# Scan of a hybrid Mamba/Hyena block: two products per group made by four scaled ACT copies instead of one POOL multiply

## The chip, the cores and the metric

One core of a Trainium2 chip runs the whole kernel as one program. Its engines work side by side, each through its own queue in order: PE (TensorE, matmuls), DVE (VectorE), ACT (ScalarE), POOL (GpSimd) and SP, which issues most transfers. The metric is the device time of one execution in microseconds (us), as the median of several runs; less is better.

## The reference

The reference is one layer on 1024 latent tokens of width 1024, with 256 context tokens: an input projection, a bidirectional chunked state-space scan (SSD) and a gated long convolution (Hyena) side by side, an output projection, and a retrieval over 16384 single-neuron experts. The change lies in the scan, which is, per direction and cut to what matters:

```python
xdt = (x * dt[..., None]).reshape(bsz, nc, q, g, r, p)
a_cum = jnp.cumsum(a, axis=-1)
l_intra = jnp.exp(segsum(a))
y_diag = jnp.einsum('bclgn,bcsgn,bgrcls,bcsgrp->bclgrp', cc, bc, l_intra, xdt)
...
y_off = jnp.einsum('bclgn,bcgrpn,bgrcl->bclgrp', cc, prev_states, jnp.exp(a_cum))
...
y = y + xs * d_skip
return group_rmsnorm(y * jax.nn.silu(z), norm_g, SSD_GROUPS)
```

There are 16 heads of 64 columns in 4 groups, and the latent tokens make 8 chunks of 128.

## The kernel before

Class `Ssd` does the scan. `run` goes through 32 steps, one for each of 4 groups in each of 8 chunks, and in each step runs `first` of the new group beside `second` of the group before.

`first` makes what `second` needs. A matmul gives the 128x128 product of the group's B and C (`cb`, in the PSUM tile `pe`). The tile `s_e`, which SP loads in `load_cum` (L559, three buffers), holds the cumulated decays of four heads in two directions, spread over all partitions; ACT subtracts and takes the magnitude head by head (L610, eight instructions a group) and then the exponential of all of it (L616). POOL makes `s_xd`, the inputs times their steps `dt`, for four heads at once, one instruction for each direction (L611, two buffers), and the skip term `s_y`, the inputs times `dskip` (L619, one buffer for a chunk). DVE masks `cb` (L617).

`second` multiplies `s_e` by the masked product on DVE (L632 and L634), has PE multiply it with `s_xd` (L639, into the PSUM tile `py`, one buffer), scales the part from the earlier states (L644, L647), adds everything into `s_y` (L648, L649) and multiplies it by the gate `s_z` on POOL (L650). After the fourth group of a chunk `done` advances the state (POOL's L503 among it), takes squares on ACT (L664), the root (L58), scales the rows (L668, a copy on ACT with a scale from a tile) and stores `s_y` (L669, to `d_ossd`). The next chunk's skip term can be written only when that store has landed.

The scan doesn't run alone. In `front` it is drawn along step by step beside the last slabs of the input projection (matmuls L199, weight split L50 and POOL's L51, convolution L229 and L235, transposes L245 with their copies L246 into `stage`), and in `mix` beside the long convolutions (matmuls L850 into the PSUM tiles `hx` and `hy`, DVE lines 766 to 845 and 993, ACT copies L777 to L823) and the key products (L1076, copied out by ACT in L1078). The order of the instructions on every engine is made by a scheduler that takes the work by priorities and simulates it; it isn't written in the code. `MB = 2` gives the projection two PSUM buffers.

Of the kernel before, what the change touches and what calls it, by code (L numbers as in the profile page):

```python
# [15 lines left out]
AF = mybir.ActivationFunctionType  # L16
# [413 lines left out]
class Ssd:  # L430
# [159 lines left out]
    def first(self, c, g, loaded):  # L590

        K, nc, wk, ps = self.K, self.K.nc, self.wk, self.ps
        x, b, bt, ct, z, prev, y = loaded
        gs = slice(g * 256, (g + 1) * 256)
        cb = ps.tile([128, 4, 128], F32, name="pe", bufs=PB)[:, 0]
        nc.tensor.matmul(cb, bt[:, g, :], ct[:, g, :], start=True, stop=True)
        e = self.e.pop(0)
        if 4 * c + g + 1 < 4 * NB:
            self.e.append(self.load_cum(4 * c + g + 1))
        xd = wk.tile([128, 2, 256], F32, name="s_xd", bufs=2)  # L600
        cbm = wk.tile([128, 2, 128], F32, name="s_cb", bufs=2)
        self.out = e, xd, cbm
        for d in range(2):
            h0 = d * 16 + g * 4
            if AD:
                (nc.vector if AD == 1 else nc.gpsimd).tensor_add(
                    e[:, d], e[:, d], self.ncum[:, c, h0:h0 + 4, None].to_broadcast([128, 4, 128]))
            else:
                for h in range(4):
                    nc.scalar.activation(e[:, d, h], e[:, d, h], AF.Abs, bias=self.ncum[:, c, h0 + h:h0 + h + 1])  # L610
            nc.gpsimd.tensor_mul(self.heads(xd[:, d]), self.heads(x[:, gs]),  # L611
                                 K.dt[:, c, h0:h0 + 4, None].to_broadcast([128, 4, 64]))
            yield
        if AD:
            nc.scalar.activation(e, e, AF.Abs)
        nc.scalar.activation(e, e, AF.Exp, scale=-1.0)  # L616
        nc.vector.tensor_mul(cbm, cb[:, None, :].to_broadcast([128, 2, 128]), self.tri)  # L617
        yield
        nc.gpsimd.tensor_mul(self.heads(y[:, gs]), self.heads(x[:, gs]),  # L619
                             self.dskip[:, g * 4:g * 4 + 4, None].to_broadcast([128, 4, 64]))  # L620
        yield

    def second(self, c, g, loaded, made):
# [1316 lines left out]
```

## Time and profile before

| what | value |
| --- | --- |
| median of 3 runs | 4127.27 us (4127.11 to 4129.32) |
| profiled execution, its own time | 4128.36 us |
| span of the profiled execution | 4126.3 us |
| mean granted TensorE clock | 0.964 |
| busy over the span: PE, DVE, ACT, POOL | 92%, 82%, 34%, 49% |

The span is the profiled execution from its first to its last instruction; a share is busy time over the span, over all stages together. The scan's groups take about a twelfth of the span, and the shares there are others than these.

### The profile page before, as it was taken

What the parts mean: (1) busy time and instruction counts of PE and PEld (TensorE: products, weight loads), DVE (VectorE), ACT (ScalarE), POOL (GpSimd) and SP (SyncE); (2) the same over time, 40 slices, a digit from 0 to 9 for tenths busy, and PEclk for the clock granted to TensorE, in tenths of its full rate; (3) what the DMA queues carried; (4) which work ended last, traced back from release to release, by engine and by line L of the source; (5) the groups of instructions that cost most, each with busy time, mean ns of one, the idle gap of its engine ahead of it and who ended that gap; (6) DMA issues with size and microseconds to landing.
All of it is one profiled execution on the core that took longest, in us unless ns stands there. A gap on an engine that the chain in (4) does not pass through costs nothing.

```text
span 4126.3 us, 60371 instructions
## 1 busy us (share of the span) xinstructions
PE 3781.7 (92%) x21993; PEld 3322.5 (81%) x21993; DVE 3394.6 (82%) x5997; ACT 1391.5 (34%) x2674; POOL 2038.8 (49%) x1643
## 2 busy tenths in 40 slices
PE   5999999999889999689999985999999999999996
PEld 3787887777788898479999985888888888788885
DVE  5666787555899787479999997799888889899897
ACT  3233333325554121232325676222322222222221
POOL 2232233244443221137524444677777777677776
PEclk9999999999799999789999998999999999999998
DMA  6333333366776445747727756799999899999997
GB/s 207 109 126 105 117 128 129 111 198 182 244 230 222 149 133 146 228 169 286 257 99 235 226 165 200 283 356 340 366 341 349 324 336 349 343 351 361 340 335 260
DMA packets 510921, 973.07 MB, mean 236 GB/s; under 512 B 33739, under 2 KB 291199, under 8 KB 506144
## 3 DMA queue, kind: packets, MB, share of 16 engines
q1 hardware_dynamic: 396864, 556.21, 40.6%
q0 software_dynamic: 110880, 405.98, 26.6%
q10 hardware_dynamic: 2880, 7.03, 0.5%
q8 instruction: 173, 2.83, 0.3%
q14 instruction: 124, 1.02, 0.1%
HBM read 822.15 MB, written 146.95 MB: 235 GB/s over the span
## 4 chain that ended last, share of the span: by engine, by line
PE 44%; DVE 22%; DMA 9%; issue 7%; POOL 5%; ACT 3%; SPq 0%; POOLq 0%; DVEq 0%; ACTq 0%
PE x_acc L1682 12%; PE x_s L1636 10%; PE mm L199 7%; DVE rows L1536 3%; PE pe L1134 2%; PE hy L850 2%; POOL rows L1512 2%; DMA s_e<-d_cum 2%; DMA x_vr<-in_peer_v_dram 2%; DVE r_e L1459 2%; PE tp L850 2%; DVE r_e L1457 2%; DMA rows<-in_peer_v_dram,ids 1%; PE hx L850 1%; DVE e_p L1549 1%
## 5 line engine op out<-in xcount | busy, mean ns | idle before, releaser
L1636 PE MATMUL x_s<-fTh,x_uh 128*128 128x320 f32 x2048 | 639.2, 312 | 14.3 <-ACT x_a L1637 14.1
L1636 PE MATMUL x_s<-fTh,x_ul 128*128 128x320 f32 x2048 | 637.1, 311 | 5.5 <-DVE x_ul L1597 5.5
L1636 PE MATMUL x_s<-fTl,x_uh 128*128 128x320 f32 x2048 | 636.9, 311 | 0.0
L1682 PE MATMUL x_acc<-x_vl,x_ah 128*128 128x512 f32 x1280 | 509.2, 399 | 28.0 <-POOL x_vl L1608 27.9
L1549 DVE SCALAR_TENSOR_TENSOR e_p<-rows,e_a,e_p 128x1024 f32<-128x1024 f32 x381 | 489.8, 1286 | 39.2 <-DMA rows<-in_peer_v_dram,ids 32.4
L1682 PE MATMUL x_acc<-x_vh,x_al 128*128 128x512 f32 x1280 | 506.5, 397 | 0.0
L1512 POOL DMA_INDIRECT rows<-in_peer_u_dram,ids x384 | 417.4, 1087 | 177.7 <-DVE rows L1536 48.3
L1536 DVE SCALAR_TENSOR_TENSOR rows<-rows,e_p 128x1024 f32<-128x1024 f32 x384 | 456.1, 1210 | 34.1 <-DMA rows<-in_peer_u_dram,ids 32.9
L1682 PE MATMUL x_acc<-x_vh,x_ah 128*128 128x512 f32 x1280 | 442.4, 397 | 38.3 <-DVE x_o L1688 16.8
L1512 POOL DMA_INDIRECT rows<-in_peer_v_dram,ids x384 | 402.4, 1048 | 140.4 <-DVE e_p L1549 62.5
L1636 PEld LDWEIGHTS x_s<-fTh,x_uh 128*128 128x128 f32 x2048 | 387.1, 189 | 30.2 <-ACT x_a L1637 19.9
L1636 PEld LDWEIGHTS x_s<-fTh,x_ul 128*128 128x128 f32 x2048 | 386.8, 189 | 15.5 <-DVE x_ul L1597 6.9
L1608 POOL TENSOR_TENSOR x_vl<-x_vr,x_vh 128x512 fp32r<-128x512 f32 x256 | 342.9, 1342 | 107.2 <-ACT x_vh L1607 103.8
L1636 PEld LDWEIGHTS x_s<-fTl,x_uh 128*128 128x128 f32 x2048 | 386.9, 189 | 9.1
L1682 PEld LDWEIGHTS x_acc<-x_vh,x_ah 128*128 128x128 f32 x1280 | 238.8, 190 | 90.5 <-DVE x_o L1688 23.1
L1682 PEld LDWEIGHTS x_acc<-x_vl,x_ah 128*128 128x128 f32 x1280 | 244.5, 191 | 81.0 <-POOL x_vl L1608 37.0
L1682 PEld LDWEIGHTS x_acc<-x_vh,x_al 128*128 128x128 f32 x1280 | 243.8, 190 | 47.9
L1597 POOL TENSOR_TENSOR x_ul<-x_raw,x_uh 128x1024 fp32r<-128x1024 f32 x57 | 140.1, 2457 | 281.5 <-ACT x_uh L1596 281.2
L1607 ACT ACTIVATE x_vh<-x_vr 128x512 fp32r<-128x512 f32 x256 | 159.9, 628 | 338.5 <-DMA x_vr<-in_peer_v_dram 265.7
L1596 ACT ACTIVATE x_uh<-x_raw 128x1024 fp32r<-128x1024 f32 x128 | 135.4, 1057 | 409.1 <-PE x_s L1636 362.3
L199 PE MATMUL mm<-xh,whi 128*128 128x512 f32 (+1 forms) x784 | 265.0, 413 | 7.4 <-DVE acc L235 3.6
L199 PE MATMUL mm<-xl,whi 128*128 128x512 f32 (+1 forms) x784 | 263.9, 411 | 7.6 <-DVE xl L51 7.6
(386 smaller groups left out, 8710.9 us busy)
## 6 DMA issues: line engine op xcount, KB each, us to landing
x_raw<-in_peer_uT_dram SPq DMA_DIRECT2D x128, 512.0 KB
x_vr<-in_peer_v_dram SPq DMA_DIRECT2D x256, 256.0 KB
d_G<-r_st SPq DMA_DIRECT2D x20, 2048.0 KB
x_g<-d_G SPq DMA_DIRECT2D x32, 1280.0 KB
wraw<-in_w_mod_dram SPq DMA_DIRECT2D x32, 1024.0 KB
wraw<-in_w_in_dram SPq DMA_DIRECT2D x24, 1024.0 KB
wk_w<-d_WK SPq DMA_DIRECT2D x24, 1024.0 KB
d_kr<-h_k SPq DMA_DIRECT2D x32, 512.0 KB
```

The costliest lines, as they stand in the source:

```text
L199: nc.tensor.matmul(p, w[:, k], x[j][:, k, t0:t0 + n], start=(k == 0 and q == 0), stop=(k == 7 and q == 2))
L850: nc.tensor.matmul(out, self.m[mats][:, tl, :], x, start=(n == 0), stop=(n == len(terms) - 1))
L1134: nc.tensor.matmul(p, a[:, k], w[:, ss], start=(k == 0 and q == 0), stop=(k == n - 1 and q == 2))
L1512: nc.gpsimd.indirect_dma_start(out=r, out_offset=None, in_=table, in_offset=bass.IndirectOffsetOnAxis(ap=ids[:, j:j + 1], axis=0))
L1536: nc.vector.scalar_tensor_tensor(r, r, 1.0, f, op0=ALU.mult, op1=ALU.mult, accum_out=d[:, j:j + 1])
L1549: nc.vector.scalar_tensor_tensor(acc, r, a[:, j:j + 1], acc, op0=ALU.mult, op1=ALU.add)
L1596: nc.scalar.activation(hi, raw, AF.Copy)
L1597: self.pace = (nc.vector if self.turn('u', UR if self.n < NE else UP) else nc.gpsimd).tensor_sub(lo, raw, hi.bitcast(F32)).ins
L1607: nc.scalar.activation(hi, raw, AF.Copy)
L1608: self.pace = nc.gpsimd.tensor_sub(lo, raw, hi.bitcast(F32)).ins
L1636: nc.tensor.matmul(s[:, :SW], w[:, k], x[:, k, ms], start=(k == 0 and q == 0), stop=(k == 7 and q == 2))
L1682: self.K.nc.tensor.matmul(p, a[x][:, bs], v[w], start=(m == 0 and q == 0), stop=(m == SC - 1 and q == 2))
```

## The change

Each of the two POOL instructions for `s_xd` becomes four ACT copies, one for a head, with that head's column of `dt` as the scale; the POOL instruction for the skip term becomes four ACT copies with the head's column of `dskip`. What is computed stays the same. The lines behind move: L616 becomes L617, and all from L623 on are two higher.

```diff
-            nc.gpsimd.tensor_mul(self.heads(xd[:, d]), self.heads(x[:, gs]),
-                                 K.dt[:, c, h0:h0 + 4, None].to_broadcast([128, 4, 64]))
+            for h in range(4):
+                hs = slice(h * 64, (h + 1) * 64)
+                nc.scalar.activation(xd[:, d, hs], x[:, gs][:, hs], AF.Copy, scale=K.dt[:, c, h0 + h:h0 + h + 1])
             yield
...
-        nc.gpsimd.tensor_mul(self.heads(y[:, gs]), self.heads(x[:, gs]),
-                             self.dskip[:, g * 4:g * 4 + 4, None].to_broadcast([128, 4, 64]))
+        for h in range(4):
+            hs = slice(g * 256 + h * 64, g * 256 + (h + 1) * 64)
+            nc.scalar.activation(y[:, hs], x[:, hs], AF.Copy, scale=self.dskip[:, g * 4 + h:g * 4 + h + 1])
         yield
```

The scheduler places the new instructions, and with them much else. On ACT, just ahead of the scan's fourth group, there stood before only the projection's work:

```order
L246 ACTIVATE stage<-tp 128x512 x2
L50 ACTIVATE whi<-wraw 128x1024
L229 ACTIVATE acc<-mm,hyb,hyw 128x1024
L246 ACTIVATE stage<-tp 128x512 x2
L610 ACTIVATE s_e<-s_e,ncum 128x128 x8
L616 ACTIVATE s_e<-s_e 128x1024
L50 ACTIVATE whi<-wraw 128x1024
```

In the changed kernel, at the same place, 32 copies stand there (for `s_xd` of two groups, and the skip term of the whole first chunk); these rows begin with the last eleven of them:

```order
L613 ACTIVATE s_xd<-s_x,dt 128x64 x2
L622 ACTIVATE s_y<-s_x,dd 128x64 x9
L246 ACTIVATE stage<-tp 128x512
L229 ACTIVATE acc<-mm,hyb,hyw 128x1024
L50 ACTIVATE whi<-wraw 128x1024
L613 ACTIVATE s_xd<-s_x,dt 128x64 x8
L610 ACTIVATE s_e<-s_e,ncum 128x128 x8
L246 ACTIVATE stage<-tp 128x512
L617 ACTIVATE s_e<-s_e 128x1024
```

The projection's `L246`, `L229` and `L50` have moved behind the copies, and eight more, for the third group, stand ahead of the next `L610`.

On ACT, at the end of the first chunk (root, scaling of the rows, first groups of the second chunk), there stood before:

```order
L58 ACT_TABLE_LOAD
L58 ACTIVATE s_n_s<-s_ss,eps 128x4
L616 ACT_TABLE_LOAD
L616 ACTIVATE s_e<-s_e 128x1024
L668 ACTIVATE s_y<-s_y,s_n_r 128x256 x4
L246 ACTIVATE stage<-tp 128x512
L610 ACTIVATE s_e<-s_e,ncum 128x128 x8
L616 ACTIVATE s_e<-s_e 128x1024
L246 ACTIVATE stage<-tp 128x512
```

In the changed kernel there stands at that place:

```order
L670 ACTIVATE s_y<-s_y,s_n_r 128x256 x4
L617 ACT_TABLE_LOAD
L617 ACTIVATE s_e<-s_e 128x1024
L613 ACTIVATE s_xd<-s_x,dt 128x64 x8
L610 ACTIVATE s_e<-s_e,ncum 128x128 x8
L622 ACTIVATE s_y<-s_x,dd 128x64 x13
L617 ACTIVATE s_e<-s_e 128x1024
L622 ACTIVATE s_y<-s_x,dd 128x64 x3
L246 ACTIVATE stage<-tp 128x512
```

Eight copies for `s_xd` have come in behind the first exponential, and thirteen of the second chunk's sixteen skip copies between the next `L610` and its exponential. On POOL the rows L611 and L619 are gone, and nothing has taken their place.

## Rows read from the trace of the kernel before

**Rows 1.** Page, section 1: busy time, share of span, instructions.
```profile
PE 3781.7 (92%) x21993; PEld 3322.5 (81%) x21993; DVE 3394.6 (82%) x5997; ACT 1391.5 (34%) x2674; POOL 2038.8 (49%) x1643
```

**Rows 2.** Stretch 930 to 1290 us: length, busy time (instructions), clock, DMA share, GB/s.
```profile
930.00:1290.00 360.00, 324.73 (x2152) 293.55 (x2151) 279.37 (x557) 204.38 (x493) 153.86 (x171) 0.92 0.69 215
```

**Rows 3.** Groups of ACT, 930 to 1290 us: count, busy us, mean ns, idle before.
```profile
L610 ACT ACTIVATE s_e<-s_e,ncum 128x128 f32<-128x128 f32 x232 | 71.1, 388 | 35.6 <-DMA s_e<-d_cum 35.6
L664 ACT ACTIVATE s_z<-s_y 128x256 f32<-128x256 f32 x32 | 13.1, 410 | 42.7 <-POOL s_y L650 42.7
L664 ACT ACTIVATION_READ_ACCUMULATOR s_z<-s_y 128x1 f32 x32 | 6.0, 188 | 0.0
L668 ACT ACTIVATE s_y<-s_y,s_n_r 128x256 f32<-128x256 f32 x32 | 13.6, 496 | 5.9 <-DVE s_n_r L59 5.9
```

**Rows 4.** Groups of DVE, same stretch and columns.
```profile
L632 DVE TENSOR_TENSOR s_e<-s_e,s_cb 128x512 f32<-128x512 f32 x29 | 23.6, 814 | 0.0
L634 DVE TENSOR_TENSOR s_e<-s_e,s_cb 128x512 f32<-128x512 f32 x29 | 23.1, 797 | 37.9 <-ACT s_e L616 37.9
L648 DVE TENSOR_TENSOR s_y<-s_y,s_t 128x256 f32<-128x256 f32 x32 | 17.2, 538 | 3.5 <-POOL s_y L619 2.7
L647 DVE TENSOR_TENSOR s_t<-s_t 128x256 f32<-128x256 f32 x32 | 16.4, 512 | 0.3
L780 DVE TENSOR_TENSOR h_tq<-h_te 128x384 f32<-128x384 f32 x7 | 6.3, 894 | 0.0
```

**Rows 5.** Groups of POOL, same stretch and columns.
```profile
L611 POOL TENSOR_TENSOR s_xd<-s_x,dt 128x256 f32<-128x256 f32 x64 | 45.6, 731 | 54.1 <-PE py L639 42.1 <-DMA s_x<-d_xs 7.4 <-issue 4.6
L619 POOL TENSOR_TENSOR s_y<-s_x,dd 128x256 f32<-128x256 f32 x32 | 26.1, 841 | 32.6 <-DMA d_ossd<-s_y 28.6 <-ACT wq_o L1078 4.0
```

**Rows 6.** Chain that ended last, 780 to 1420 us, by line.
```profile
by line: PE mm L199 18.4%; DMA s_e<-d_cum 11.0%; ACT s_e L610 5.6%; PE pe L1134 4.8%; issue 4.4%; PE py L639 3.9%; PE st L508 3.2%; PE hy L850 3.1%; DVE h_m L993 2.8%; DVE s_e L632 2.1%; PE hx L850 2.1%; ACT s_e L616 1.8%; DVE h_a L766 1.5%
```

**Rows 7.** Timeline of ACT: start us, us, engine, line, count.
```profile
1070.59 1.70 ACT L668 ACTIVATE s_y<-s_y,s_n_r 128x256 f32<-128x256 f32 x4 [5.93 <-DVE s_n_r L59]
1072.20 2.43 ACT L610 ACTIVATE s_e<-s_e,ncum 128x128 f32<-128x128 f32 x8
```

**Rows 8.** Timeline around the first copies of the scan.
```profile
931.13 1.06 ACT L50 ACTIVATE whi<-wraw 128x1024 fp32r<-128x1024 f32 x1 [2.26 <-PE mm L199]
932.10 1.19 ACT L229 ACTIVATE acc<-mm,hyb,hyw 128x1024 f32<-128x1024 f32 x1
...
932.68 0.61 POOL L611 TENSOR_TENSOR s_xd<-s_x,dt 128x256 f32<-128x256 f32 x1 [7.41 <-DMA s_x<-d_xs]
```

**Rows 9.** Waits, 930 to 1290 us: us in total, times, longest.
```profile
DVE s_e L634 <- ACT s_e L616: 37.9, 18, 6.5
ACT s_e L610 <- DMA s_e<-d_cum: 35.6, 17, 5.4
```

**Rows 10.** Timeline around 1080 us.
```profile
1080.44 2.89 DVE L780 TENSOR_TENSOR h_tq<-h_te 128x384 f32<-128x384 f32 x1
1080.60 2.31 POOL L619 TENSOR_TENSOR s_y<-s_x,dd 128x256 f32<-128x256 f32 x4
...
1080.98 1.95 PE L850 MATMUL hy<-h_m,dft_i 128*128 128x128 f32 x16
```

**Rows 11.** Instructions of single tiles: ns min/median/max, first and last start us.
```profile
L634 DVE TENSOR_TENSOR s_e<-s_e,s_cb x32: 678/692/2372, 817.9 to 1262.1; 128x512 f32<-128x512 f32 x32
L632 DVE TENSOR_TENSOR s_e<-s_e,s_cb x32: 677/685/2393, 818.5 to 1263.1; 128x512 f32<-128x512 f32 x32
...
L648 DVE TENSOR_TENSOR s_y<-s_y,s_t x32: 408/425/1484, 960.9 to 1279.7; 128x256 f32<-128x256 f32 x32
...
L647 DVE TENSOR_TENSOR s_t<-s_t x32: 404/423/1211, 960.5 to 1279.2; 128x256 f32<-128x256 f32 x32
...
L780 DVE TENSOR_TENSOR h_tq<-h_te x7: 543/549/2892, 1046.3 to 1281.5; 128x384 f32<-128x384 f32 x7
...
L639 PE MATMUL py<-s_xd,s_e x512: 217/275/447, 936.8 to 1282.8; 128*128 128x64 f32 x171
```

## The prediction

> **What bounds the kernel now.** The page gives TensorE (PE) 92% and VectorE (DVE) 82% of the span, ACT 34%, POOL 49% [rows 1], but such shares average over stages. The change touches one stage, the scan, whose groups run from about 930 to 1290 us, so I read that stage by itself. The row of the stretch [rows 2] shows PE busy 324.7 us of 360 at a granted clock of 0.92, DVE 279.4, ACT 204.4 and POOL 153.9. PE has only 35 us of holes, because the order puts other matmuls (the last projection slabs, then the long convolutions and the key products) between the scan's own. The stage is therefore a bundle of coupled queues with PE nearly full; a delay costs time only when it reaches PE after those fillers are used up.
>
> Next come the waits of each engine there. ACT's groups [rows 3] show what a scan group does: eight `Abs` of 128 columns (L610), one `Exp` of 1024 (L616), then the multiply on DVE. ACT waits 35.6 us for the load of `s_e`, and 42.7 us before the squares of L664, for POOL's multiply. DVE in turn waits 37.9 us for the `Exp` before L634 [rows 4]: here ACT's chain is what comes last. POOL's two groups that go away, L611 and L619, are busy 45.6 and 26.1 us, and POOL sat idle for others 54 and 33 us before them [rows 5]; POOL is not what the stage waits for. The chain that ended last, from 780 to 1420 us, says the same: after the projection's matmuls its largest shares are the load of `s_e` (11.0%) and ACT's L610 (5.6%), and neither POOL line is among those listed [rows 6].
>
> **The change, part by part.** Removed: 64 + 32 POOL multiplies, 45.6 + 26.1 = 71.7 us of POOL. Added: 64 x 4 + 32 x 4 = 384 ACT copies of 128x64.
>
> *Price of a copy.* No ACT row has this shape. Eight L610 of 128 columns take 2.43 us and four L668 of 256 columns, a copy with a scale from a tile as the new ones are, take 1.70 [rows 7]. Less the mean of the last one [rows 3], start to start is (2.43 - 0.388)/7 = 0.292 and (1.70 - 0.496)/3 = 0.401 us. The 128 columns between them cost 0.109, so 64 columns less than L610 give 0.292 - 0.055 = 0.24 us, of which about 0.18 does not depend on the width. Bounds: the one-column read of the accumulator, 0.188, below [rows 3], and 0.292 above; 72 to 112 us in all. I take 0.24: 92 us for 384, 2.0 us for the eight copies of a group, 3.9 for the sixteen of a chunk's skip term. ACT in the stretch becomes 204 + 92 = 296 of 360 us, 82%.
>
> The fixed 0.18 us is where a rule and the rows differ. The Trainium skill (Perfetto Trace Analysis, Optimizing Scalar/DVE Operations) puts the access overhead of a Scalar instruction on SBUF at about 93 ns, and advises larger instructions when an engine is saturated; with 0.093 in place of 0.18 the addition would be an estimated 57 us instead of 92. The advice speaks against cutting one multiply into four copies, and the rows make the cut dearer than the page does.
>
> *Where the copies stand.* The order of the changed kernel, not the source, decides what waits.
>
> (a) Start. All sixteen copies of the first two groups' inputs and the sixteen of the first skip term stand in a row on ACT, behind the load of `s_x`. POOL waited for that load until 932.7 us [rows 8]. Thirty-two copies end 7.7 us later, at 940.4; behind them now queue the `stage` copy, the convolution's L229 and the weight split L50, which ran at 931 to 933 [rows 8] and now end near 943. PE works on from a second weight buffer and a second PSUM buffer, which is the cover. Nothing if it holds, 9 us if it does not (the delay of L229); I take 3.
>
> (b) Between `Abs` and `Exp`. Most groups have their eight copies behind their own `Exp`, in front of the next `Abs`, which waits for a load anyway. In eight groups the copies stand between a group's `Abs` and its `Exp`, and in two the skip copies do (13 and 12 of 16): 8 x 2.0 + 25 x 0.24 = 22 us by which an `Exp` comes later. What queues behind is that `Exp`, and DVE's L634 waits for it. In the trace before, 18 of the 29 L634 of the stretch waited for ACT [rows 4, 9]. I take 18/29 of 22 = 14 us; nothing and 22 are the bounds.
>
> (c) The other five skip blocks, 5 x 3.9 = 20 us, wait for the store of the chunk before to land (28.6 us of POOL's idle time [rows 5]); POOL could sit there, ACT has other work behind it, such as the key products' copies L1078 and those of the inverse transform, for which PE waits. Part of the store's time has passed by then, since an `Exp` or an `Abs` stands in between. Nothing to 20; I take a third, 6 us. The first copies of a group also wait for `py` of two groups before to release `s_xd`, as POOL's did for 42.1 us [rows 5]; but the next `Abs` waits for a load issued after that same `py`, so this wait is a shared one and costs nothing unless something else is behind it.
>
> (d) Relief of DVE. DVE's instructions with both inputs in SBUF stretch when POOL runs: the 128x384 add L780 took 2.89 us beside four L619 that ran 2.31 us [rows 10], against a median of 0.549 [rows 11]. Mean less median, times count, for five groups [rows 4, 11]: L632 3.7, L634 3.0, L648 3.6, L647 2.8, L780 2.4, together 15.7 us (the rows' medians are of all instances of a line). The removed groups are 71.7 of POOL's 153.9 us, 47%, so 7 us, and some in groups not listed: I take 8, counted whole, with nothing and 16 as bounds.
>
> Sum: 3 + 14 + 6 - 8 = +15 us. The profiled execution took 4128.4 us, 1.1 above the median of the runs, so the median is forecast at 4127.3 + 15 = 4142 us. The bounds give 4127.3 - 16 = 4111 and 4127.3 + 9 + 22 + 20 = 4178. The order also differs later, in the expert stage, where the scores' matmuls (L1636) and those of the routing swap places. The instructions are the same and PE is full with either; I price that at nothing.
>
> **Rivals.** About 0.2%, 8 us, is what a measurement of this kernel can tell from no change.
>
> *No change: the copies fill holes.* ACT's 35.6 us of waits for `s_e` came in 17 pieces [rows 9], 2.1 us each, just the length of one group's copies. And the new order has moved fillers forward: before the scan's last `py` stand 65 more matmuls of the long convolution and 16 more key products, about 81 x 0.24 = 19 us of PE work (16 trace rows, eight matmuls, take 1.95 us [rows 10]). If the scan ends 19 us later and PE is full meanwhile, nothing is lost. Against it: the holes are placed by transfers, and an in-order queue at 82% rarely meets them. Time: (a) alone less part of (d), 4127.
>
> *Faster: DVE was the limit.* DVE has 80.6 us free in the stretch, so it isn't the limit throughout; but the relief may come just where it is. If (a) to (c) are covered and (d) counts by its upper bound, the time is 4111. The point from which it decides: the `Exp` mustn't come later than DVE is ready for it, so L634's wait must stay at or under 38 us. The Trainium skill (SBUF — State Buffer, Who interferes with whom) says that a DVE instruction with two SBUF inputs and a POOL instruction that reads SBUF exclude each other, and that ACT never waits on anyone; by that rule moving work from POOL to ACT can only free DVE. The 2.89 us of L780 agree with the first half.
>
> *Much slower: ACT becomes the bound.* If ACT's waits can't be filled, the whole 92 us less 8 lengthen the stretch: about 4211. For it speaks that the copies' own waits sit on the same queue; against it that 155 us of ACT are free and that most blocks stand behind their `Exp`. It needs ACT over 95% busy in the stage.
>
> **Numbers.** Forecast 0.49, no change 0.22, faster 0.20, ACT-bound 0.09. The range 4111 to 4178 takes in the first three and leaves out the last and the outer part of the third. Slower is 0.49 + 0.09 = 0.58; the forecast's own range is 4136 to 4178.
>
> **What would show it** (lines by the numbers of the kernel before). The copies: 384 ACT rows of 128x64, union near 0.24 us each; if 0.30, ACT is over 85%. (a): L50 near 942 instead of 931, and a PE hole of a few us soon after. (b): L634's wait for ACT rising from 37.9 to about 50 us. (c): waits of PE for L1078 and for the inverse transform's copies, rising by some 6 us together. (d): means of L632, L634, L648 and L647 falling to within 50 ns of their medians. The last `py` (L639) starting at 1300 to 1320 us instead of 1282.8 [rows 11]. The forecast is wrong if PE's holes in the stage stay at 35 us or shrink while the scan ends later: then fillers covered it. It is wrong too if the difference turns up after 1800 us, where only the order of the same instructions changed.

## The result and the profile after

The changed kernel took 4152.3 us (median of 6 runs, 4143.1 to 4163.9) against 4127.5 for the kernel before on the same chips, a ratio of 1.0053 [1.0037, 1.0069]: 25 us slower. The forecast was 4142, from a scan that takes 15 us longer. The profiled execution took 4143.1 us with a span of 4141.4, so it shows 15 of the 25 us.

The scan's stretch has become what the prediction said of ACT, and not what it said of the time. This is the row that answers to [rows 2]:

```profile
930.00:1290.00 360.00, 318.29 (x2224) 291.71 (x2224) 270.19 (x578) 294.47 (x879) 92.10 (x77) 0.95 0.71 222
```

ACT is busy 294.5 of 360 us (204.4 before), POOL 92.1 (153.9), DVE 270.2 (279.4). PE has 360 - 318.3 = 41.7 us of holes, 6.4 more than before, but 72 more of its rows lie in the stretch, at a granted clock of 0.95 instead of 0.92. The groups of ACT in that stretch, with the columns of [rows 3]:

```profile
L613 ACT ACTIVATE s_xd<-s_x,dt 128x64 f32<-128x64 f32 x256 | 64.9, 336 | 12.7 <-PE py L641 8.7 <-DMA s_x<-d_xs 4.0
L622 ACT ACTIVATE s_y<-s_x,dd 128x64 f32<-128x64 f32 x128 | 32.1, 334 | 5.5 <-DMA d_ossd<-s_y 5.5
```

And the groups of DVE that answer to [rows 4]:

```profile
L634 DVE TENSOR_TENSOR s_e<-s_e,s_cb 128x512 f32<-128x512 f32 x29 | 21.4, 739 | 0.0
L636 DVE TENSOR_TENSOR s_e<-s_e,s_cb 128x512 f32<-128x512 f32 x29 | 20.9, 719 | 31.7 <-ACT s_e L617 31.6
L649 DVE TENSOR_TENSOR s_t<-s_t 128x256 f32<-128x256 f32 x32 | 15.4, 481 | 0.5
```

The 384 copies keep ACT busy 97.0 us, 0.253 each. The DVE products have become shorter (0.814 to 0.739 us, 0.797 to 0.719 [rows 4]), and the wait for the exponential has fallen from 37.9 to 31.6 us, where 50 had been forecast. The start, in a timeline of ACT that answers to [rows 8]:

```profile
935.71 2.25 ACT L622 ACTIVATE s_y<-s_x,dd 128x64 f32<-128x64 f32 x9
937.85 0.58 ACT L246 ACTIVATE stage<-tp 128x512 f32<-128x512 f32 x1
938.33 1.20 ACT L229 ACTIVATE acc<-mm,hyb,hyw 128x1024 f32<-128x1024 f32 x1
939.42 1.06 ACT L50 ACTIVATE whi<-wraw 128x1024 fp32r<-128x1024 f32 x1
```

L229 and L50 come 6 and 8 us later than before (some 9 and 11 were foretold), yet PE is busy 69.58 us of the stretch from 930 to 1000, and was 69.57 before. How far the kernel has come is best read at single lines, with their first and last start. Of the kernel before: the output projection's part that runs in the mix (L1134), and the expert stage's second matmul (L1682):

```profile
L1134 PE MATMUL pe<-wo_h,ot_l x192: 387/392/481, 1323.8 to 1655.3; 128*128 128x512 f32 x192
...
L1682 PE MATMUL x_acc<-x_vh,x_ah x1280: 387/390/795, 2576.0 to 4102.7; 128*128 128x512 f32 x183
```

Of the changed kernel, the same view of the scan's product and of the same two lines:

```profile
L641 PE MATMUL py<-s_xd,s_e x512: 217/275/476, 934.6 to 1291.6; 128*128 128x64 f32 x171
...
L1136 PE MATMUL pe<-wo_h,ot_l x192: 387/392/628, 1320.5 to 1649.3; 128*128 128x512 f32 x192
...
L1684 PE MATMUL x_acc<-x_vh,x_ah x1280: 387/392/795, 2572.2 to 4117.1; 128*128 128x512 f32 x183
```

The scan's last product starts 8.8 us later than before [rows 11], where the forecast had 17 to 37, but the mix ends 6.0 us earlier and the expert stage begins 3.8 us earlier; only in that stage does the kernel fall behind, by 14.4 us at its last product. From the first start of L1682 or L1684 to the end of the span it takes 4126.3 - 2576.0 = 1550.3 us before and 4141.4 - 2572.2 = 1569.2 after. I call this stretch the stage. The change doesn't touch its instructions. The stretch between the mix's end and the stage takes 920.7 us before and 922.9 after.

### The profile page after: what moved, and what is told of

The parts are those of the page before. It is cut to its first block, busy times and chain, and to the rows that moved or that the text cites. A ratio compares the mean times of both kernels' runs of the same rounds, so it can differ in the third digit from the quotient of the medians.

```text
span 4141.4 us, 60620 instructions
## 1 busy us (share of the span) xinstructions
PE 3776.5 (91%) x21993; PEld 3321.2 (80%) x21993; DVE 3360.7 (81%) x5997; ACT 1481.1 (36%) x3060; POOL 1980.4 (48%) x1547
## 4 chain that ended last, share of the span: by engine, by line
PE 47%; DVE 21%; DMA 9%; issue 6%; POOL 4%; ACT 3%; SPq 0%; POOLq 0%; DVEq 0%; ACTq 0%
PE x_acc L1684 14%; PE x_s L1638 11%; PE mm L199 7%; DVE rows L1538 3%; PE pe L1136 2%; PE hy L852 2%; DMA x_vr<-in_peer_v_dram 2%; DVE r_e L1461 2%; PE tp L852 1%; PE hx L852 1%; DMA rows<-in_peer_u_dram,ids 1%; DVE r_e L1459 1%; POOL rows L1514 1%; DMA rows<-in_peer_v_dram,ids 1%; DVE r_tmp L1348 1%
## 5 line engine op out<-in xcount | busy, mean ns | idle before, releaser
L1684 PE MATMUL x_acc<-x_vl,x_ah 128*128 128x512 f32 x1280 | 514.0, 402 | 31.0 <-POOL x_vl L1610 30.8
L1684 PE MATMUL x_acc<-x_vh,x_al 128*128 128x512 f32 x1280 | 509.3, 399 | 0.0
L1684 PE MATMUL x_acc<-x_vh,x_ah 128*128 128x512 f32 x1280 | 440.1, 398 | 39.3 <-DVE x_o L1690 14.8
L1684 PEld LDWEIGHTS x_acc<-x_vl,x_ah 128*128 128x128 f32 x1280 | 246.2, 192 | 86.9 <-POOL x_vl L1610 41.7
L1684 PEld LDWEIGHTS x_acc<-x_vh,x_ah 128*128 128x128 f32 x1280 | 238.6, 190 | 90.7 <-DVE x_o L1690 19.5
L1684 PEld LDWEIGHTS x_acc<-x_vh,x_al 128*128 128x128 f32 x1280 | 246.1, 192 | 48.4
```

The lines of the kernel that those rows point to most:

```text
L1684: self.K.nc.tensor.matmul(p, a[x][:, bs], v[w], start=(m == 0 and q == 0), stop=(m == SC - 1 and q == 2))
```

## The experiments

Two theories stood against each other. *Order*: the scan's change costs nothing, and the loss comes from the expert stage, where the scheduler lays out the same instructions in another order. *Scan*: the copies cost the 25 us, one way or another. In what follows the order is that of PE from the first `x_acc` matmul on, 7633 rows in the compiled program. Before has order A and the changed kernel order C, with the same row at the same place (counted from the end) in 4589 of the 7633. The letter stands for more than PE: between before and changed the stage's rows in the traces differ on DVE (1043 of 1588 at the same place), ACT (471 of 652) and POOL (834 of 951) too, and kernels with the same letter have these alike (with TR 0.91 but for some ten rows of DVE). So the runs price the order of the whole stage, and not that of PE alone. All the kernels made for the experiments but the one with both loads have the line numbers of the changed kernel.

| kernel | order | mix ends, us | stage, us | median, us | ratio to before |
| --- | --- | --- | --- | --- | --- |
| before | A | 1655.3 | 1550.3 | 4127.5 | |
| changed | C | 1649.3 | 1569.2 | 4152.3 | 1.0053 [1.0037, 1.0069] |
| before, barrier | B | 1654.5 | 1576.5 | 4157.4 | 1.0077 [1.0063, 1.0091] |
| changed, barrier | near B | 1651.0 | 1574.1 | 4144.8 | 1.0042 [1.0029, 1.0056] |
| inputs only | B | 1663.0 | 1572.0 | 4158.4 | 1.0087 [1.0073, 1.0100] |
| inputs only, barrier | near C | 1659.9 | 1568.9 | 4163.0 | 1.0094 [1.0079, 1.0110] |
| skip term only | F | 1661.9 | 1572.8 | 4167.6 | 1.0098 [1.0083, 1.0112] |
| both loads | C | 1651.6 | 1580.8 | 4153.4 | 1.0055 [1.0042, 1.0068] |
| copies behind the exponential | B | 1657.0 | 1570.9 | 4157.9 | 1.0072 [1.0059, 1.0085] |
| products left out | D | 1658.3 | 1558.1 | 4144.9 | 1.0036 [1.0023, 1.0048] |
| changed, TR 0.91 | A | 1648.6 | 1553.9 | 4128.3 | 0.9992 [0.9980, 1.0003] |
| before, TR 0.91 | C | 1649.5 | 1576.8 | 4150.4 | 1.0047 [1.0032, 1.0061] |
| changed, one transfer | E | 1651.1 | 1574.5 | 4145.9 | 1.0045 [1.0028, 1.0063] |
| changed, two transfers | D | 1645.1 | 1563.1 | 4136.1 | 1.0024 [1.0013, 1.0034] |

The mix's end is the last start of L1134 (L1136), the stage is worked out as above from each profiled execution, and the ratio is to runs of before on the same chip. What is left of each span, from the mix's end to the stage's start, takes 918 to 931 us.

**A barrier between mix and experts.** In both kernels, one line:

```diff
     mix(K, scan)
+    tc.strict_bb_all_engine_barrier()
     back(K)
```

> The kernel before with a barrier of all engines between the mix and the expert block. With the barrier the compiler's scheduler lays out the 9984 expert matmuls in another order (call it B; before has A, the changed kernel has C). Theory order: the 25 us came from the expert stage, whose instructions are the same and only stand in another order, so a barrier that changes nothing but that order may also move the time by tens of us, up or down: 4100 to 4165 us, and the stretch from the first x_acc matmul to the end is not 1550 us as before. Theory scan (the copies themselves cost the 25 us): the barrier costs only its own drain, 4128 to 4140 us, and that stretch stays within 5 us of 1550.

> The changed kernel with the same barrier; its expert matmuls then stand in order B almost exactly as in the run beside it, so the difference of the two is the scan's change alone. Theory order: 2 to 10 us shorter than the kernel before with the barrier, the whole difference reached by the end of the mix, and the expert stages of the two within 4 us of each other. Theory scan: 15 to 30 us longer than the kernel before with the barrier.

The barrier alone made the kernel before 32 us slower. Its mix ends within a microsecond of before's; the row of its second expert matmul, with first and last start:

```profile
L1684 PE MATMUL x_acc<-x_vh,x_ah x1280: 387/390/797, 2579.2 to 4132.3; 128*128 128x512 f32 x183
```

The same row of the changed kernel with the barrier:

```profile
L1684 PE MATMUL x_acc<-x_vh,x_ah x1280: 387/390/795, 2579.0 to 4118.9; 128*128 128x512 f32 x183
```

Until the stage it lost 3.2 us, in the stage 26.2, with the scan untouched. With the change it was 12.6 us faster by the medians, somewhat beyond the 2 to 10 expected, though the two profiled executions differ by 2.6 us of span only, and their mixes by 3.5. The two stages, 1576.5 and 1574.1 us, are alike in sum only: PE's last product starts 13.4 us earlier with the change, and what follows the last matmul, work of the other engines and the last store, takes 33 us instead of 23. The orders are not quite the same here (6913 of 7633 rows, and all the others lie in the last sixth of the stage), so this pair doesn't say what the scan is worth. The 15 to 30 us more of the scan theory show neither in the medians nor at the mix's end.

**One half alone.** The inputs' copies without the skip copies, without and with the barrier, and the skip copies alone (edit not shown, it is the other half of the change). The first, against the kernel before:

```diff
-            nc.gpsimd.tensor_mul(self.heads(xd[:, d]), self.heads(x[:, gs]),
-                                 K.dt[:, c, h0:h0 + 4, None].to_broadcast([128, 4, 64]))
+            for h in range(4):
+                hs = slice(h * 64, (h + 1) * 64)
+                nc.scalar.activation(xd[:, d, hs], x[:, gs][:, hs], AF.Copy, scale=K.dt[:, c, h0 + h:h0 + h + 1])
```

> Only the inputs times their steps are made on ACT (256 copies, 65 us of ACT by the 0.253 us of a copy); the skip term stays on GpSimd. Without any barrier its expert matmuls come out in order B, row for row as in the kernel before with the barrier. Theory order: its stretch from the first x_acc matmul to the end equals that of the kernel before with the barrier within 4 us, and its mix ends 0 to 8 us earlier than before's. Theory scan: two thirds of the loss, so 10 to 20 us over before.

> The same half of the change, with the barrier: now the expert matmuls stand in order C, within a few rows of the changed kernel's. Theory order: its stretch from the first x_acc matmul to the end is the changed kernel's, 1569 us, within 4 us, whatever the scan does, and so differs from that of the same scan without a barrier. Theory scan: it is as long as that of the same scan without a barrier, and 10 to 20 us of loss stand in the scan.

> The other half of the change alone: only the skip term is made by ACT copies (128), the inputs times their steps stay on GpSimd. The mix's end is read at the last matmul of L1134 of before (1655.7 us there; 6 us earlier in the changed kernel, 7.6 later in the run with the 256 copies alone). If the two halves add up, it stands here 10 to 17 us earlier than before's; if POOL's relief of DVE counts only when all of it is gone, 0 to 4 us either way. The expert matmuls come out in an order of their own, nearest to C: theory order gives an expert stage of 1560 to 1580 us, and no loss in the scan; theory scan gives a loss of 5 to 10 us in the scan.

The stages went by the order, within 4.5 us for B (4 expected) and 0.3 for C (here the barrier's stage is near C: 6789 rows of 7633, the others all in its first quarter). But the mix ended 7.7 us later than before's with the inputs alone and 6.6 later with the skip term alone, while with both it ends 6.0 earlier. By the order theory each half was expected to save or to cost nothing there, so it missed both, and the 6.6 lies in the 5 to 10 us that the scan theory gave the skip term. The skip term alone is the slowest kernel of all: of its 39 us of span over before, 6.6 lie in the mix, 9.9 between mix and stage and 22.5 in the stage. The halves don't add up, and the order of the scan's own stretch is another than before's and the changed kernel's in all three; the next runs speak against a cost of the work itself.

**Both loads, and neither.** POOL makes the products into a scratch tile besides ACT's copies; and, in the other kernel, nobody makes them (the steps and the skip weights are left out of the result):

```diff
+            nc.gpsimd.tensor_mul(self.heads(self.wk.tile([128, 256], F32, name="s_du", bufs=1)), self.heads(x[:, gs]), K.dt[:, c, h0:h0 + 4, None].to_broadcast([128, 4, 64]))
...
+        nc.gpsimd.tensor_mul(self.heads(self.wk.tile([128, 256], F32, name="s_du", bufs=1)), self.heads(x[:, gs]), self.dskip[:, g * 4:g * 4 + 4, None].to_broadcast([128, 4, 64]))
```

```diff
-            nc.gpsimd.tensor_mul(self.heads(xd[:, d]), self.heads(x[:, gs]),
-                                 K.dt[:, c, h0:h0 + 4, None].to_broadcast([128, 4, 64]))
+            pass
...
-                nc.tensor.matmul(py[:, h * 64:(h + 1) * 64], e[:, d, h], xd[:, d, h * 64:(h + 1) * 64],
+                nc.tensor.matmul(py[:, h * 64:(h + 1) * 64], e[:, d, h], x[:, gs][:, h * 64:(h + 1) * 64],
...
-        nc.vector.tensor_add(y[:, gs], y[:, gs], t[:, :256])
+        nc.vector.tensor_add(y[:, gs], x[:, gs], t[:, :256])
```

> The changed kernel, and POOL makes the three products as well, into a scratch tile that nobody reads, so that ACT and POOL both carry the work. The expert matmuls keep order C row for row. Theory relief (the scan is 6 us earlier because POOL no longer slows DVE): the mix ends 5 to 20 us later than in the changed kernel, and the DVE products on s_e are back at about 0.80 us from 0.73. If the relief is worth nothing: within 2 us of the changed kernel. Theory order: the expert stage is 1569 us within 4 in both cases.

> Neither engine makes the products: the matmuls take the inputs as they are and the sum starts from the inputs, so the steps and the skip weights are left out of the result. It shows the most that moving this work could win. If the scan's stretch is set by ACT or POOL, the mix ends 15 us or more earlier than in the kernel before; if it is PE's own work that sets it, 6 to 12 us earlier, no more than a few us better than the changed kernel. The expert matmuls come out in yet another order (that of no kernel so far): theory order says only that the stage lies at 1550 to 1580 us.

With both loads (line numbers two higher than in the changed kernel), the row of the stretch from 930 to 1290 us:

```profile
930.00:1290.00 360.00, 318.52 (x2197) 291.37 (x2195) 284.80 (x572) 292.11 (x871) 154.78 (x170) 0.94 0.72 220
```

Two groups of DVE in it:

```profile
L636 DVE TENSOR_TENSOR s_e<-s_e,s_cb 128x512 f32<-128x512 f32 x29 | 25.8, 888 | 0.0
L638 DVE TENSOR_TENSOR s_e<-s_e,s_cb 128x512 f32<-128x512 f32 x29 | 24.4, 842 | 31.6 <-ACT s_e L618 31.4
```

The line with which the mix ends, first and last start:

```profile
L1138 PE MATMUL pe<-wo_h,ot_l x192: 387/392/628, 1322.8 to 1651.6; 128*128 128x512 f32 x192
```

With the products left out, the row of the same stretch:

```profile
930.00:1290.00 360.00, 314.07 (x2147) 286.60 (x2147) 264.88 (x558) 199.90 (x485) 86.33 (x75) 0.93 0.72 216
```

And the line with which its mix ends:

```profile
L1136 PE MATMUL pe<-wo_h,ot_l x192: 387/393/628, 1329.6 to 1658.3; 128*128 128x512 f32 x192
```

POOL's load is back at 154.8 us and DVE's products are slower than they ever were (0.888 us), so the contention is real; yet the mix ends only 2.3 us later than in the changed kernel. This pair is a clean one: up to the mix's end PE has the same 8954 rows in the same order in both, and ACT and DVE theirs but for a few neighbours exchanged, so little but POOL's 96 multiplies differs. The two kernels with a tiny transfer (the last experiment) keep that order and the changed kernel's scan, and their mixes end at 1651.1 and 1645.1 us; 2.3 us can't be told from nothing in single executions. And with 92 us of ACT and 68 of POOL less than with both loads, the mix ends 6.7 us *later*, 3.0 later than before's, where 6 us earlier or more had been expected whatever set its length; the order of the scan's stretch is another one there. What moving this work wins in the mix doesn't show: where the mix ends (1645 to 1663 us over all the kernels) doesn't go with what ACT and POOL carry. The stage with both loads, 1580.8, missed its 1565 to 1573, in an execution that was the slowest of its five (4160.3 us; the others 4148.5 to 4154.4): the same order varies by some 10 us.

**The copies behind the exponential.**

```diff
-            for h in range(4):
-                hs = slice(h * 64, (h + 1) * 64)
-                nc.scalar.activation(xd[:, d, hs], x[:, gs][:, hs], AF.Copy, scale=K.dt[:, c, h0 + h:h0 + h + 1])
+            pass
...
         nc.scalar.activation(e, e, AF.Exp, scale=-1.0)
+        for d, h in ((d, h) for d in range(2) for h in range(4)):
+            nc.scalar.activation(xd[:, d, h * 64:(h + 1) * 64], x[:, gs][:, h * 64:(h + 1) * 64], AF.Copy, scale=K.dt[:, c, d * 16 + g * 4 + h:d * 16 + g * 4 + h + 1])
```

> The changed kernel with the eight copies of a group for s_xd written behind the exponential instead of between the magnitudes and it. The prediction's step (b), that the copies keep DVE waiting for the exponential, gives a mix end 5 to 14 us earlier than the changed kernel's, and a shorter wait of DVE for the exponential than 31.6 us. If that place costs nothing: within 3 us. Its expert matmuls come out in order B, so theory order gives an expert stage of 1572 to 1577 us.

The wait that step (b) charged didn't get shorter, and the mix ends 7.7 us later than the changed kernel's, outside both of the ranges given, with another order in the scan's stretch. The stage, 1570.9 us, lies 1.1 under its range. The wait row (the exponential stands in L615 here):

```profile
DVE s_e L636 <- ACT s_e L615: 35.8, 18, 3.8
```

**The two orders exchanged.** `TR` is the rate at which the output projection's steps draw the long convolution's along, behind the scan. At 0.91 the scheduler gives each of the two kernels the other's expert order:

```diff
-TR = 0.9
+TR = 0.91
```

> The changed kernel with TR at 0.91 instead of 0.90, the rate at which the output projection in the mix draws convolution steps along; no work is added or removed. With it the expert matmuls stand row for row in order A, the order of the kernel before. Theory order: the expert stage takes 1550 us as in before (1546 to 1556), and the time is before's less what the mix saves, 4117 to 4130 us, so 22 to 35 us under the changed kernel by a number that touches neither the scan nor the experts. Theory scan (the copies cost the loss): the time stays within 8 us of the changed kernel's 4152.

> The kernel before, its products still on GpSimd, with the same TR of 0.91. Now its expert matmuls stand row for row in order C, the order of the changed kernel. Theory order: the expert stage takes 1567 to 1582 us as in the changed kernel, and the time is 4147 to 4162 us, slower than before by as much as the change made it. Theory scan: 4122 to 4134 us, no different from before.

The orders agree in all but 43 (A) and 26 (C) of the 7633 rows. The changed kernel, in A, has lost its loss; the kernel before, in C, has it. Stages and medians of both lie in the ranges of the order theory and outside those of the scan theory. The row of the expert stage's stretch, of the changed kernel with TR 0.91 (first start of L1684 at 2575.1):

```profile
2575.00:4129.00 1554.00, 1471.26 (x7632) 1287.37 (x7632) 1371.48 (x1590) 402.76 (x654) 1118.41 (x951) 0.98 0.91 335
```

PE's waits in it (us, times, longest):

```profile
PE x_acc L1684 <- POOL x_vl L1610: 27.6, 15, 5.7
PE x_acc L1684 <- DVE x_o L1690: 13.8, 13, 2.5
PE x_acc L1684 <- ACT x_ah L50: 11.3, 1, 11.3
PE x_acc L1684 <- ACT x_vh L1609: 9.3, 6, 2.4
PE x_s L1638 <- ACT x_a L1639: 8.7, 9, 2.4
```

The same two views of the kernel before with TR 0.91 (first start of L1684 at 2567.5), the stretch:

```profile
2568.00:4144.00 1576.00, 1480.66 (x7632) 1293.82 (x7631) 1371.58 (x1589) 401.52 (x653) 1123.59 (x951) 0.97 0.90 330
```

And the waits:

```profile
PE x_acc L1684 <- POOL x_vl L1610: 28.0, 20, 6.9
PE x_acc L1684 <- ACT x_vh L1609: 18.7, 10, 2.8
PE x_acc L1684 <- DVE x_o L1690: 14.3, 11, 3.4
PE x_acc L1684 <- ACT x_ah L50: 11.1, 1, 11.1
PE x_s L1638 <- ACT x_a L1639: 10.6, 7, 2.5
```

In either order the scan's change is worth nothing that can be told: 4128.3 against 4130.3 us in A (the runs of before on that chip), 4152.3 against 4150.4 in C. Nor does it show in the mix: with TR 0.91 that ends at 1648.6 and 1649.5 us, so the rate alone moved the end of before's mix by as much as the change had. The order is worth 20 us with the old scan and 24 with the new one. PE is the busiest engine of the stage; its 22 us in this pair divide into idle time, 1554 - 1471.3 = 82.7 against 1576 - 1480.7 = 95.3 us, and busy time for the same number of rows, 9.4 us more at a clock of 0.97 instead of 0.98. Before and the changed kernel divide likewise. The row of the stage of before:

```profile
2576.00:4126.00 1550.00, 1467.75 (x7632) 1283.13 (x7632) 1377.63 (x1589) 403.58 (x653) 1117.79 (x951) 0.98 0.91 336
```

And of the changed kernel:

```profile
2572.00:4141.00 1569.00, 1477.04 (x7632) 1289.48 (x7632) 1367.32 (x1589) 402.15 (x654) 1119.13 (x951) 0.98 0.90 332
```

That is 82.3 against 92.0 us idle and 9.3 us more busy. In C, PE comes more often to a matmul whose operand isn't ready: the low half of a weight from POOL (`x_vl`, 15 and 20 times in the crossed pair, 16 and 23 in before and changed), and its high half from ACT (`x_vh`, 6 and 10 times, 8 and 9). Of the 12 us that the rows of waits differ by in the crossed pair, 9.4 are for `x_vh`.

The 9.3 us more of busy time come with the clock. The trace holds the stretches at which it was granted at 1.2 instead of 2.4 GHz (a clock of 0.50); here is the sum over all of them from the stage's first product to its last, in the kernel before, where they are 8:

```profile
sum 37.55, PE 30.58 PEld 24.02 DVE 21.53 ACT 7.73 POOL 27.84; mean PE 3.82 PEld 3.00 DVE 2.69 ACT 0.97 POOL 3.48
```

And in the changed kernel, where they are 11:

```profile
sum 58.51, PE 47.31 PEld 38.10 DVE 33.99 ACT 11.39 POOL 41.01; mean PE 4.30 PEld 3.46 DVE 3.09 ACT 1.04 POOL 3.73
```

PE was busy 16.7 us longer at the lower level. Its 128x512 matmuls start 0.43 us apart there (from 2678.73 to 2679.16 us) and 0.23 at a clock of 1.00 (from 2669.14 to 2669.37), so half of the 16.7, some 8.4 us, is the clock's price, and it is nearly all of the 9.3. Busy time less half of what was busy at the lower level is 1450 to 1454 us in all fourteen kernels, whatever their order. Ahead of the falls within the stage PE had gaps: in the changed kernel it waited 4.45 us for `x_o` until 2678.07 us, and from 2678.51 on the clock was 0.50. So the order costs time twice, in the waits themselves and in the lower clock behind them; that the waits bring the falls is read from this sequence, and no run varied one without the other.

**Two more orders.** One or two tiny transfers ahead of the routing, read by nobody:

```diff
-        self.iota = mid.tile([128, 128], F32, name="iota_f")
+        self.iota = mid.tile([128, 128], F32, name="iota_f"); tiny = mid.tile([128, 16], F32, name="tiny"); self.K.nc.sync.dma_start(tiny, self.K.i["b_modT"])
```

> The changed kernel with one tiny transfer more (8 KB on SP, read by nobody) ahead of the routing. It draws yet another order of the expert matmuls, E. Theory order says that the time goes with the order and not with the transfer: an expert stage somewhere at 1550 to 1582 us and a total of 4125 to 4165 us; under 4120 us would show that order A isn't near the low end of what this program can draw. Theory scan: 4152 us, as the changed kernel, within 8.

> The same with two such transfers. Its expert matmuls come out in order D, row for row that of the kernel that left the products out, whose expert stage took 1558 us. Theory order: 1553 to 1566 us in that stage and a total of 4128 to 4146 us, though one transfer more than in the run beside it, which has another order. Theory scan: 4152 us within 8.

Only the second separates the theories. One transfer gives 1574.5 us for the new order E, but its 4145.9 us lie within the 8 us of 4152 that the scan theory allowed, and the range of the order theory was as wide as all stages seen. Two transfers give 1563.1 for D, which the kernel without the products has row for row (1558.1), and 4136.1 us, as the order theory said and outside the range of the other. The kernel with one transfer more is 10 us faster than the other. Of the six orders none is shorter than A.

## Why the prediction was right in its number and wrong in its reasons

The direction, the size (25 us for 15) and the range came out, and that was luck: the steps that made them mostly did not.

- *Price of the copies.* 0.24 us forecast, 0.253 measured, 97.0 us for 92; ACT 82% busy, as worked out. By the 93 ns of overhead that the Trainium skill (Perfetto Trace Analysis, Optimizing Scalar/DVE Operations) gives a Scalar instruction on SBUF it would have been an estimated 57; the trace bears out the dearer reading.
- *(a) Start, +3.* The projection's work on ACT was put off as described, and the cover held: PE's busy time up to 1000 us is unchanged. The term is zero.
- *(b) Copies ahead of the exponential, +14.* The wait fell by 6.3 us instead of rising by 12, and moving all the copies behind the exponential gained nothing. The step took a copy's time as a delay of the exponential. ACT had waits of its own there for the load of `s_e`, and the rival without change had named them: they are 31.0 us now, 35.6 before. That the copies lie in them is the likely reason and not shown.
- *(c) Skip blocks ahead of PE's evacuations, +6.* The waits rose as described: PE's for L1078's copies (now L1080's) from 1.9 to 4.4 us, those of the inverse transform (`hy`) for ACT's from 2.6 to 6.1, and its holes by 6.4. But the rival's 81 fillers, 162 rows in the trace at two a matmul, do start ahead of the scan's last product, some 19 us of PE's work by the prediction's 0.24, and that product comes 8.8 us later only. The mix ends earlier. A hole in one place, with the other work done sooner, isn't a loss.
- *(d) Relief of DVE, -8.* DVE's busy time fell by 9.2 us, and the means of its four lines came to within 16 to 58 ns of their medians, where 50 had been forecast. The Trainium skill (SBUF — State Buffer, Who interferes with whom) says that a DVE instruction with two SBUF inputs and a POOL instruction that reads SBUF contend for ports that only one of them holds at a time; the runs agree in kind: 0.739 us without POOL's products, 0.888 with them, in the same order. For the mix's end that was 2.3 us in the one pair, no more than executions of one order differ by.
- *The order of the expert stage, priced at nothing.* This step failed, and it is the whole result. "The instructions are the same and PE is full with either": PE is 94 to 95% busy there, and the same instructions take 1550 to 1554 us in order A, 1558 to 1563 in D and 1569 to 1581 in the others. The prediction named the test that would refute it, a difference after 1800 us, and that is what the trace shows.

So the scan's own part came out as the first rival had it, no change, and the number came right by the term that was priced at nothing. Which engine's order it is that makes PE wait less in A, and which of the scheduler's decisions tips from one order to another, stays open; that 0.01 in a rate or a transfer that nobody reads does it is all that was shown. The halves' later mix ends are open as well: the kernel with both loads, which has more to do than either half and keeps the changed kernel's order, speaks for an order there too, but neither half was run in another's scan order. No kernel beat the one before: the changed one in order A equals it (0.9992 [0.9980, 1.0003]).

## What to carry to other kernels

Where a scheduler makes the order, an edit has two prices: its own, and that of the order that it draws for everything behind it, here 8 to 30 us of 4130 in a stage that the edit doesn't touch. Read where the two traces part before explaining a difference, and look for an edit without any work that exchanges the two orders: the crossed pair separates the prices with two more kernels. The kernel before had the best of the six draws seen here, so a change worth nothing showed as a loss.

## What the runs showed of the hardware that was not expected

Taking 68 us off POOL and 92 us off ACT in a stretch of 360 us (neither load against both) didn't shorten the mix; PE was 87 to 88% busy in that stretch, and the two have different orders there. POOL's 96 multiplies, added in an otherwise equal order, made DVE's products on `s_e` 20% longer (0.739 to 0.888 us). In a stage where PE is 94 to 95% busy, some 10 us more of gaps went with 17 us more of PE's work at a clock of 0.50, so half of the loss stands in longer rows and not in idle time. And executions of one and the same program differ by more in some kernels than in others: the kernel before with the barrier ran at 4154.0 to 4160.1 us in five runs and the changed kernel with it at 4135.5 to 4154.9. In the changed kernel the fastest run has the highest mean clock and the slowest the lowest (0.965 at 4143.1 us, 0.960 at 4163.9), but the kernel before with the barrier shows no such link (0.960 at 4157.4, 0.963 at 4160.1); what sets the spread stays open.
